# A decoder step on one core: 28 instead of 20 blocks of u split by ScalarE and GpSimd, and dots ordered behind the one-hot rows

## The chip, the cores and the metric

The kernel runs on one core of one Trainium2 chip. The metric is the device time of one execution in microseconds (us), from three runs of the kernel before. Engine names are those of the profile: PE is TensorE, PEld its weight loads, DVE is VectorE, ACT is ScalarE, POOL is GpSimd, SP is SyncE. SP and POOL also issue transfers (DMA); those issued by one engine go out in its order.

## The reference

One inference step of a decoder with two layers, for a prompt group and a small sample group. Layer 0 mixes tokens with a delta rule and a linear recurrence, layer 1 with windowed attention. After each mixer comes the same block, PEER, and the change lies in it alone:

```python
def block(tb):                                             # 128 tokens and more
    q = (tb @ w_q).reshape(PEER_BLOCK, PEER_HEADS, 2, PEER_D_SUB)
    s = jnp.einsum('thcd,hcnd->thcn', q, sub_keys)         # 8 heads x 2 halves x 128 keys
    s_top, i_top = lax.top_k(s, PEER_TOPK)                 # 16 of each half
    cand = s_top[:, :, 0, :, None] + s_top[:, :, 1, None, :]
    best, pos = lax.top_k(cand, PEER_TOPK)                 # 16 experts of 16384 per head
    expert = take(cand_idx, pos); gate = softmax(best)
    act = gelu(einsum('td,thkd->thk', tb, u_tab[expert]))
    return einsum('thk,thkd->td', gate * act, v_tab[expert])
```

A token meets 128 experts, each with a row of u and a row of v of 1024 numbers.

## The kernel before

For three token tiles of 128 (384 columns) the kernel doesn't gather: it multiplies by the whole table u, in 128 blocks of 128 experts, masks the result with a dense gate matrix, and multiplies by the whole of v. For a fourth tile and the sample rows, experts are fetched by row (gathers) and reduced on DVE (dots). `peer(layer)` does this, once per layer, in stages.

**Scores.** 16 half-heads (hc): a projection by a block of w_q on PE, a float32 product with the keys (`psc`, line 445), copies by ACT (`q`, `scs`, `ss`), top-16 on DVE (`topk_half`, lines 267 to 271). Beside them, `presplit_load` and `presplit_pool` (lines 104 to 116) prepare the first NPOOL blocks of u: a matrix product in float32 accuracy takes each block as two float16 halves, high and low. SP loads the block (`gst`, three buffers), ACT scales it and copies the high half (into `gpr`, two buffers), POOL subtracts to get the low half (line 114), and SP stores both in DRAM (`PW`).

**Pairs and u steps.** A u step (`u_step`) is 24 matmuls of 128x384 on PE (`pu`, lines 91 to 93: high by high, high by low, low by high) and a gelu on ACT. Its block comes from `ublock` (line 143): one of the first NPOOL is loaded from PW, ready (`wpr`); a later one is loaded raw (`wst`), and ACT makes the high half (`wh`, line 77) and DVE the low half (`wl`, line 86) just ahead of PE. Three buffers hold `wst` and `wpr` together, two hold `wh` and `wl`. While PE does u steps, DVE forms the 50 candidate pairs of each token and head and takes the best 16 (`topk_pairs`, lines 267 to 318), first for the samples and the gathered tile, then for dense tile 0. It ends in `ij` (line 503); PE transposes it (`pt`), and DVE and ACT form `lt`.

**Gates.** Twelve stages, four for each dense tile. In one stage DVE writes 16 one-hot rows (`oh`, lines 530 to 533, in groups of four instructions, two buffers of groups), PE multiplies them in 64 small matmuls (`pg`, lines 537 and 538; 768 in all), ACT copies the results to `stage`, and 2 MB go to DRAM (`GD`). Each stage has u steps in the program beside it (UG 3), and the pairs of the next dense tile come after stages 3 and 7. After each stage three steps of `g_ustep` follow (GU 3): one gather on POOL (line 390, 512 KB, three buffers `row`) and, from the third step on, one dot on DVE (line 397). That gives 36 gathers and 34 dots in the gates, 10 of the dots in stages 0 to 3 and 24 in stages 4 to 11.

**Main.** 128 blocks of v with the rest of the u steps; `yps` (line 654) is its product. 79 u steps and two matmuls of the next come before its first matmul.

What stands in which order on an engine is not the order of the program: a scheduler simulates the engines and issues what it finds ready, so it may place a dot far ahead of the stage that it was written behind. `behind(ins)` (line 124) binds what is written under it to be issued behind given instructions, and `last_on(V)` is the last DVE instruction written so far.

Of the kernel before, what the change touches and what calls it, by code (L numbers as in the profile page):

```python
# [70 lines left out]
class Kern:  # L71
# [249 lines left out]
    def peer(self, layer):  # L321
        nc, tc, A = self.nc, self.tc, self.A
        V, S, G, T = nc.vector, nc.scalar, nc.gpsimd, nc.tensor
# [49 lines left out]
        def run_u(k):  # L373
            for _ in range(k):
                u_step()
# [11 lines left out]
        def gather(src, n):  # L387
            k = korder[n]
            r = rows[0].tile([P, D], F32, name="row")
            G.indirect_dma_start(out=r, out_offset=None, in_=src,  # L390
                                 in_offset=bass.IndirectOffsetOnAxis(ap=elist[:, k:k + 1], axis=0))
            return r

        def g_dot(n):
            k = korder[n]
            u = ubuf.pop(n)
            V.tensor_tensor_reduce(u, u, self.xtok[:, 0] if k < P else xrep, 1.0, 0.0, OP.mult, OP.add,  # L397
                                   hd[:, k:k + 1])
            if n % GRP == GRP - 1:
                a = korder[n - GRP + 1]  # L400
                S.activation(wgt[:, a:a + GRP], hd[:, a:a + GRP], AF.Gelu_apprx_tanh)
                V.tensor_mul(wgt[:, a:a + GRP], wgt[:, a:a + GRP], glist[:, a:a + GRP])

        def g_ustep():
            if gn[0] < NK:
                ubuf[gn[0]] = gather(urows, gn[0])
                gn[0] += 1
            if gn[1] < NK and gn[1] + 2 < gn[0] or gn[0] == NK and gn[1] < NK:
                g_dot(gn[1])
                gn[1] += 1  # L410
# [64 lines left out]
        with tc.tile_pool(name="gates", bufs=1, reuse_waits="tile") as gp, \  # L475
# [12 lines left out]
            def pairs(t):  # L488
                ev = tp.tile([P, 8, TOPK], F32, name="ev")
                gt = tp.tile([P, 8, TOPK], F32, name="gt")  # L490
                self.topk_pairs(tp, st[:, t], ix[:, t], P, 8, ev, gt)
                lts[t] = ev, gt

            def pairs_t(t):

                ev, gt = lts[t]
                ei = tp.tile([P, P], I32, name="ei")
                V.tensor_copy(ei, ev.rearrange("p a b -> p (a b)"))
                e2 = tp.tile([P, 2, P], I32, name="e2")
                V.tensor_scalar(e2[:, 0], ei, 7, None, op0=OP.logical_shift_right)  # L500
                V.tensor_scalar(e2[:, 1], ei, 127, None, op0=OP.bitwise_and)
                ij = tp.tile([P, 2, P], F32, name="ij")
                V.tensor_copy(ij, e2)
                pt = psum.tile([P, 4, P], F32, name="pt")
                T.transpose(pt[:, 0], ij[:, 0], self.ident)
                T.transpose(pt[:, 1], ij[:, 1], self.ident)
                T.transpose(pt[:, 2], gt.rearrange("p a b -> p (a b)"), self.ident)
                lt = tp.tile([P, 4, P], F16, name="lt", bufs=2)
                self.copy(lt[:, 0:2], pt[:, 0:2])
                V.tensor_scalar(lt[:, 2], pt[:, 2], SCG, None, op0=OP.mult)  # L510
                V.scalar_tensor_tensor(lt[:, 3], pt[:, 2], SCG, lt[:, 2], op0=OP.mult, op1=OP.subtract)
                lts[t] = lt

            def gates(t, part, us):

                lt = lts[t]
                stage = gp.tile([P, P, TG], F32, name="stage")
                run_u(us - 1)
                order = self.last_on(S)
                for t4 in range(0, TG, 4):  # L520
                    if t4 % 8 == 0:

                        sl = slice(part * TG + t4, part * TG + t4 + 8)

                        def tok(k):
                            return lt[:, k, sl].rearrange("p (a b) -> p a b", b=2)[:, :, None, :].to_broadcast([P, 4, P, 2])

                        io = self.iota2[:, None].to_broadcast([P, 4, P, 2])
                        oh = gp.tile([P, 4, 4, P, 2], F16, name="oh", bufs=2)
                        V.tensor_tensor(oh[:, 0], io, tok(1), op=OP.is_equal)  # L530
                        V.tensor_tensor(oh[:, 1], io, tok(0), op=OP.is_equal)
                        V.tensor_mul(oh[:, 2], oh[:, 1], tok(2))
                        V.tensor_mul(oh[:, 3], oh[:, 1], tok(3))
                    pg = psum.tile([P, 4, P], F32, name="pg", bufs=4)
                    for k in range(4):
                        q, r = divmod(t4 % 8 + k, 2)
                        T.matmul(pg[:, k], oh[:, 0, q, :, r], oh[:, 2, q, :, r], start=True, stop=False)
                        T.matmul(pg[:, k], oh[:, 0, q, :, r], oh[:, 3, q, :, r], start=False, stop=True)  # L538
                    with self.behind(order):
                        self.copy(stage[:, :, t4:t4 + 4].rearrange("p i t -> p t i"), pg)  # L540
                    order = []
                    if t4 == TG // 2:
                        run_u(1)
                nc.scalar.dma_start(GD[P // TG * t + part], stage)
# [20 lines left out]
            for k in range(12):  # L565
                gates(k // 4, k % 4, self.UG)
                acc[0] += self.GU
                while acc[0] >= 1:
                    g_ustep()
                    acc[0] -= 1  # L570
                if k % 4 == 3 and k < 11:
                    run_u(self.UP)
                    pairs(k // 4 + 1)
                    pairs_t(k // 4 + 1)
# [995 lines left out]
    def run(self):  # L1570
        nc, tc, A = self.nc, self.tc, self.A
        with ExitStack() as ctx:
            self.constants(ctx)
            self.RING, self.NSP, self.UG, self.GU, self.ROWS = 50, 32, 3, 3, 9
            self.UP = 7
            dp = ctx.enter_context(tc.tile_pool(name="scratch", bufs=1, space=bass.MemoryType.DRAM))
            self.GD = dp.tile([12, P, P, 32], F32, name="GD")
            self.NPRE, self.NPOOL = (0, 0), 20
            self.PW = dp.tile([2, max(self.NPRE) + self.NPOOL, P, 2, KB, P], F16, name="PW")
            self.AD = dp.tile([self.NSP, P, ND], F32, name="AD")  # L1580
            self.wst = ctx.enter_context(tc.tile_pool(name="wst", bufs=3))
            self.wsp = ctx.enter_context(tc.tile_pool(name="wsp", bufs=2))
            xp = ctx.enter_context(tc.tile_pool(name="x", bufs=1))
            self.xtok = xp.tile([P, 2, D], F32, name="xtok")
            self.xh = xp.tile([P, KB, NT], F16, name="xh")
            self.xl = xp.tile([P, KB, NT], F16, name="xl")
            self.eq = xp.tile([P, 2, 256], F32, name="eq")
            with tc.tile_pool(name="xin", bufs=1) as q:
                xT = q.tile([P, KB, NT], F32, name="xT")
                self.wfirst = {20: self.wblock(A["wab"][20])}  # L1590
                for kb in range(KB):
                    if kb == 4:
                        self.wfirst[4] = self.wblock(A["wab"][4])
                    nc.sync.dma_start(xT[:, kb], A["xT"][:, kb])
                    self.split(self.xh[:, kb], self.xl[:, kb], xT[:, kb])
            self.bd = dp.tile([16, P, LB], F32, name="bd")
            self.sbd = dp.tile([P, P], F32, name="sbd")
            xd0 = dp.tile([NT, D], F32, name="xd0")
            xd1 = dp.tile([3 * P, D], F32, name="xd1")
            self.xd = [A["xtok"], xd1]  # L1600
            with ExitStack() as c:
                pre = self.mixer_ab(c)
                self.presplit(pre, 0, self.NPRE[0])
            self.xd = [xd0, xd1]
            self.peer(0)
            with ExitStack() as c:
                pre = self.mixer_c(c)
                self.presplit(pre, 1, self.NPRE[1])
            self.peer(1)
# [141 lines left out]
```

## Time and profile before

| what | value |
|---|---|
| runs | 2965.84, 2963.49, 2955.86 us; median 2963.49 us |
| profiled execution, its own time | 2954.78 us |
| its span in the trace | 2953.1 us |
| PE busy | 2824.2 us (96%) |
| DVE busy | 2501.0 us (85%) |
| ACT busy | 1351.7 us (46%) |
| POOL busy | 956.7 us (32%) |
| moved | 811.33 MB, mean 275 GB/s |
| mean granted PE clock | 0.989 |
| chain that ended last | PE 59%, DMA 13%, DVE 12%, ACT 7%, issue 6% |

Busy shares are means over stages with different limits; a span outside the instructions of 1.7 us lies between the execution's own time and the trace. A matmul is in flight longer than its distance to the next (0.33 us against 0.16), so a busy PE isn't a PE at its peak: where PE's steps matter, distances of starts are taken. In layer 0 the scores lie at about 356 to 470 us, the pairs to 592, the gates to 835; `yps` begins at 852.3.

### The profile page before, as it was taken

How to read it: one execution, taken by the hardware profiler on the slowest of the kernel's cores; microseconds unless marked ns; L12 is line 12 of the kernel's file. 1: busy time of each engine (PE TensorE's matmuls, PEld its weight loads, DVE VectorE, ACT ScalarE, POOL GpSimd, SP SyncE). 2: the span in 40 equal slices, each digit the busy share in tenths (PEclk: the TensorE clock that was granted, in tenths of full speed). 3: DMA queues.
4: the chain of work that ended last, by engine and by line, in shares of the span. 5: the costliest groups of instructions: out<-in, count | busy, mean ns of one | idle time of the engine just before them, and what ended most of it. 6: DMA issues, size and time to landing. Idle time of an engine off the chain costs nothing.

```text
span 2953.1 us, 49153 instructions
## 1 busy us (share of the span) xinstructions
PE 2824.2 (96%) x18198; PEld 1714.9 (58%) x18198; DVE 2501.0 (85%) x5483; ACT 1351.7 (46%) x2127; POOL 956.7 (32%) x702
## 2 busy tenths in 40 slices
PE   8999999899999999999998999989999999999998
PEld 7787686466655555544447658646665555554443
DVE  6755789999878898889985869999988889888998
ACT  4733473266743333333435747236674333333332
POOL 2300151310034554445530014140005455444652
PEclk9999999999999999999999999999999999999999
DMA  4223495975699999999984348686569999999996
GB/s 134 71 83 129 147 330 193 311 253 199 225 380 357 372 362 369 360 324 375 354 289 162 106 144 299 238 296 223 211 252 382 355 374 363 355 347 346 330 368 223
DMA packets 320324, 811.33 MB, mean 275 GB/s; under 512 B 28099, under 2 KB 150411, under 8 KB 316244
## 3 DMA queue, kind: packets, MB, share of 16 engines
q1 hardware_dynamic: 229228, 455.37, 44.7%
q0 software_dynamic: 78336, 285.25, 26.0%
q10 hardware_dynamic: 12520, 67.58, 6.2%
q8 instruction: 142, 2.33, 0.3%
q14 instruction: 98, 0.80, 0.1%
HBM read 707.25 MB, written 99.46 MB: 273 GB/s over the span
## 4 chain that ended last, share of the span: by engine, by line
PE 59%; DMA 13%; DVE 12%; ACT 7%; issue 6%; POOL 3%; ACTq 0%; SPq 0%; POOLq 0%; DVEq 0%
PE yps L654 24%; PE pu L93 7%; PE pu L91 7%; PE pu L92 7%; DMA row<-in_u_rows,elist 3%; DMA gl<-GD 3%; ACT stage L77 2%; POOL row L390 2%; DMA gst<-in_uT 1%; DVE row L397 1%; ACT wh L77 1%; DVE wl L86 1%; PE psg L1034 1%; DMA row<-in_v_rows 1%; PE pg L538 1%
## 5 line engine op out<-in xcount | busy, mean ns | idle before, releaser
L654 PE MATMUL yps<-vv,vw 128*128 128x512 f16 x4536 | 1008.4, 380 | 10.4 <-DVE vv L86 8.4
L654 PEld LDWEIGHTS <-vw 128*128 128x128 f16 x4608 | 450.7, 98 | 546.1 <-issue 19.6
L390 POOL DMA_INDIRECT row<-in_v_rows,elist x272 | 398.1, 1463 | 836.3 <-ACT stage L77 425.0
L93 PE MATMUL pu<-xh,wl 128*128 128x384 f16 x1728 | 565.8, 329 | 28.5 <-DVE wl L86 28.1
L91 PE MATMUL pu<-xh,wh 128*128 128x384 f16 x1728 | 567.5, 328 | 21.7 <-ACT wh L77 21.7
L92 PE MATMUL pu<-xl,wh 128*128 128x384 f16 x1728 | 566.9, 328 | 0.0
L390 POOL DMA_INDIRECT row<-in_u_rows,elist x272 | 385.8, 1418 | 509.5 <-DVE yac L592 129.3
L86 DVE SCALAR_TENSOR_TENSOR wl<-wst,wh 128x1024 f16<-128x1024 f32 x284 | 351.3, 1240 | 165.8 <-ACT wh L77 151.7
L77 ACT ACTIVATE wh<-wst 128x1024 f16<-128x1024 f32 x284 | 299.3, 1054 | 403.5 <-PE pu L92 293.3
L77 ACT ACTIVATE vv<-row 128x1024 f16<-128x1024 f32 x252 | 264.2, 1051 | 369.6 <-PE yps L654 291.7
L91 PEld LDWEIGHTS <-wh 128*128 128x128 f16 x2816 | 279.9, 99 | 166.3 <-ACT wh L77 39.1
L93 PEld LDWEIGHTS <-wl 128*128 128x128 f16 x2816 | 277.5, 99 | 168.5 <-DVE wl L86 38.5
L86 DVE SCALAR_TENSOR_TENSOR vv<-row,vv 128x1024 f16<-128x1024 f32 x252 | 307.7, 1222 | 63.6 <-ACT vv L77 60.2
L92 PEld LDWEIGHTS <-wh 128*128 128x128 f16 x2816 | 277.7, 99 | 132.8 <-issue 5.9
L592 DVE SCALAR_TENSOR_TENSOR yac<-row,wgt,yac 128x1024 f32<-128x1024 f32 x268 | 343.3, 1281 | 8.7 <-DMA row<-in_v_rows,elist 6.7
L397 DVE CUSTOM_DVE_ANT_0 row<-row,xtok 128x1024 f32<-128x1024 f32 x256 | 308.4, 1220 | 20.7 <-DMA row<-in_u_rows,elist 20.5
L77 ACT ACTIVATE vw<-act 128x384 f16<-128x384 f32 x256 | 129.3, 514 | 226.8 <-PE yps L654 191.5
L77 ACT ACTIVATE stage<-pg 128x512 f32<-128x512 f32 x192 | 182.7, 1104 | 71.1 <-DMA GD<-stage 42.9
L366 ACT ACTIVATE act<-pu 128x384 f32<-128x384 f32 x256 | 121.7, 477 | 87.0 <-PE pu L93 86.1
L84 DVE TENSOR_TENSOR vw<-act,vw 128x384 f16<-128x384 f32 x256 | 139.3, 553 | 13.8 <-ACT vw L77 13.4
L640 DVE TENSOR_TENSOR act<-act,gl 128x384 f32<-128x384 f32 x256 | 127.6, 552 | 11.2 <-DMA gl<-GD 9.1
L92 PE MATMUL pq<-xl,wh 128*128 128x264 f16 (+1 forms) x480 | 132.9, 277 | 0.7 <-DVE xl L84 0.7
(502 smaller groups left out, 4138.8 us busy)
## 6 DMA issues: line engine op xcount, KB each, us to landing
row<-in_v_rows SPq DMA_DIRECT2D x256, 512.0 KB
wst<-in_uT SPq DMA_DIRECT2D x216, 512.0 KB
GD<-stage ACTq DMA_DIRECT2D x24, 2048.0 KB
gl<-GD SPq DMA_DIRECT2D x64, 768.0 KB
gst<-in_uT SPq DMA_DIRECT2D x40, 512.0 KB
PW<-gpr SPq DMA_DIRECT2D x40, 512.0 KB
wpr<-PW SPq DMA_DIRECT2D x40, 512.0 KB
wst<-in_wq SPq DMA_DIRECT2D x32, 512.0 KB
```

Of the source, the lines that this page charges most:

```text
L77: self.nc.scalar.activation(out, in_, AF.Copy, scale=scale)
L84: eng.tensor_sub(lo, src, hi)
L86: eng.scalar_tensor_tensor(lo, src, scale, hi, op0=OP.mult, op1=OP.subtract)
L91: mm(out, wh, xh, start=start, stop=False)
L92: mm(out, wh, xl, start=False, stop=False)
L93: mm(out, wl, xh, start=False, stop=stop)
L366: S.activation(t, ps[:, 0:ND], AF.Gelu_apprx_tanh, scale=1.0 / SCW)
L390: G.indirect_dma_start(out=r, out_offset=None, in_=src, in_offset=bass.IndirectOffsetOnAxis(ap=elist[:, k:k + 1], axis=0))
L397: V.tensor_tensor_reduce(u, u, self.xtok[:, 0] if k < P else xrep, 1.0, 0.0, OP.mult, OP.add, hd[:, k:k + 1])
L592: V.scalar_tensor_tensor(dst, vbuf.pop(n), wgt[:, k:k + 1], dst, op0=OP.mult, op1=OP.add)
L640: V.tensor_mul(a6, a6, gl)
L654: T.matmul(yps[t][:, o], w[:, a, c], v[:, b, o], start=x == 0 and k == 0, stop=x == P - 1 and k == 2)
```

## The change

NPOOL goes from 20 to 28. Blocks 20 to 27 of u are then prepared in the scores by ACT and POOL and read from PW, and no longer split by ACT and DVE in front of their u step. And what DVE does in the `g_ustep` calls behind gate stages 4 to 11 is bound behind the last DVE instruction of that stage, its last one-hot product (line 533). The gathers themselves, on POOL, are not bound, and stages 0 to 3 not either.

```diff
--- before.py
+++ after.py
@@ -566,7 +566,8 @@
                 gates(k // 4, k % 4, self.UG)
                 acc[0] += self.GU
                 while acc[0] >= 1:
-                    g_ustep()
+                    with self.behind(self.last_on(V) if k >= 4 else []):
+                        g_ustep()
                     acc[0] -= 1
                 if k % 4 == 3 and k < 11:
                     run_u(self.UP)
@@ -1575,7 +1576,7 @@
             self.UP = 7
             dp = ctx.enter_context(tc.tile_pool(name="scratch", bufs=1, space=bass.MemoryType.DRAM))
             self.GD = dp.tile([12, P, P, 32], F32, name="GD")
-            self.NPRE, self.NPOOL = (0, 0), 20
+            self.NPRE, self.NPOOL = (0, 0), 28
             self.PW = dp.tile([2, max(self.NPRE) + self.NPOOL, P, 2, KB, P], F16, name="PW")
             self.AD = dp.tile([self.NSP, P, ND], F32, name="AD")
             self.wst = ctx.enter_context(tc.tile_pool(name="wst", bufs=3))
```

Three places show how the order of the engines changes, in layer 0; layer 1 is alike. Rows give the line, the operation and output<-input.

ACT, end of the scores, before: `q`, `scs` and `ss` of the last half-heads, then the table and the first gelu of a u step.

```order
L77 ACTIVATE q<-pq 128x256
L77 ACTIVATE q<-pq 128x264
L77 ACTIVATE scs<-psc 128x512
L77 ACTIVATE ss<-psc 128x8
L77 ACTIVATE q<-pq 128x256
L77 ACTIVATE q<-pq 128x264
L77 ACTIVATE scs<-psc 128x512
L77 ACTIVATE ss<-psc 128x8
L77 ACTIVATE scs<-psc 128x512
L77 ACTIVATE ss<-psc 128x8
L366 ACT_TABLE_LOAD
L366 ACTIVATE act<-pu 128x384
```

ACT at the same place now:

```order
L77 ACTIVATE q<-pq 128x256
L77 ACTIVATE q<-pq 128x264
L77 ACTIVATE gst<-gst 128x1024
L77 ACTIVATE scs<-psc 128x512
L77 ACTIVATE ss<-psc 128x8
L77 ACTIVATE gpr<-gst 128x1024
L77 ACTIVATE gst<-gst 128x1024
L77 ACTIVATE gpr<-gst 128x1024
L366 ACT_TABLE_LOAD
L366 ACTIVATE act<-pu 128x384
L77 ACTIVATE scs<-psc 128x512
L77 ACTIVATE ss<-psc 128x8
```

Before, the last `gpr` stands four half-heads earlier; now two blocks go in each of these half-heads, and the last `scs` stands behind the first gelu instead of ahead of it.

DVE, the first one-hot rows of stage 0, before (`wl` is a low half, L397 a dot):

```order
L86 SCALAR_TENSOR_TENSOR wl<-wst,wh 128x1024
L269 MATCH_REPLACE cwork<-best_7597,cand_7568 128x50
L510 TENSOR_SCALAR lt<-pt 128x128
L530 TENSOR_TENSOR oh<-iota_65,lt 128x1024
L531 TENSOR_TENSOR oh<-iota_65,lt 128x1024
L530 TENSOR_TENSOR oh<-iota_65,lt 128x1024
L531 TENSOR_TENSOR oh<-iota_65,lt 128x1024
L270 MAX best_7597<-cwork 128x8
L511 SCALAR_TENSOR_TENSOR lt<-pt,lt 128x128
L397 ISA row,hd<-row,xtok 128x1024
L397 ISA hd 128x1
L532 TENSOR_TENSOR oh<-oh,lt 128x1024
```

DVE, the same place now:

```order
L290 TENSOR_TENSOR cand_8782<-st 128x8x8
L304 CAST pf_7667<-pos_7622 128x128
L510 TENSOR_SCALAR lt<-pt 128x128
L530 TENSOR_TENSOR oh<-iota_65,lt 128x1024
L531 TENSOR_TENSOR oh<-iota_65,lt 128x1024
L530 TENSOR_TENSOR oh<-iota_65,lt 128x1024
L531 TENSOR_TENSOR oh<-iota_65,lt 128x1024
L311 TENSOR_TENSOR eq_7669<-pf_7667,lperm 128x256
L316 TENSOR_REDUCE gsum_7685<-gexp_7664 128x8
L511 SCALAR_TENSOR_TENSOR lt<-pt,lt 128x128
L267 MAX best_8811<-cand_8782 128x8 x8
L532 TENSOR_TENSOR oh<-oh,lt 128x1024 x2
```

Between the last top-16 of the scores and the first row L530 there stood 29 dots and 8 `wl`; now there are 10 dots and no `wl`. The first `wl`, that of block 28, comes 28 one-hot instructions later.

DVE, the last one-hot rows of the seventh stage (stage 6), before:

```order
L530 TENSOR_TENSOR oh<-iota_65,lt 128x1024
L531 TENSOR_TENSOR oh<-iota_65,lt 128x1024
L503 CAST ij<-e_8857 128x256
L532 TENSOR_TENSOR oh<-oh,lt 128x1024
L533 TENSOR_TENSOR oh<-oh,lt 128x1024
L530 TENSOR_TENSOR oh<-iota_65,lt 128x1024
L531 TENSOR_TENSOR oh<-iota_65,lt 128x1024
L532 TENSOR_TENSOR oh<-oh,lt 128x1024
L533 TENSOR_TENSOR oh<-oh,lt 128x1024
L86 SCALAR_TENSOR_TENSOR wl<-wst,wh 128x1024
L510 TENSOR_SCALAR lt<-pt 128x128
L530 TENSOR_TENSOR oh<-iota_65,lt 128x1024
```

DVE, the last one-hot rows of the same stage now:

```order
L530 TENSOR_TENSOR oh<-iota_65,lt 128x1024
L531 TENSOR_TENSOR oh<-iota_65,lt 128x1024
L532 TENSOR_TENSOR oh<-oh,lt 128x1024
L533 TENSOR_TENSOR oh<-oh,lt 128x1024
L397 ISA row,hd<-row,xtok 128x1024
L397 ISA hd 128x1
L397 ISA row,hd<-row,xtok 128x1024
L397 ISA hd 128x1
L397 ISA row,hd<-row,xtok 128x1024
L397 ISA hd 128x1
L86 SCALAR_TENSOR_TENSOR wl<-wst,wh 128x1024
L530 TENSOR_TENSOR oh<-iota_65,lt 128x1024
```

Three dots now stand in a row behind the last L533 of a stage, ahead of the next `wl` and the next stage's rows. Counted to the `wl` of block 53: before, 88 one-hot instructions, 36 dots, 33 `wl` and 358 others since the scores; now 136, 22, 25 and 364.

## Rows read from the trace of the kernel before

**Rows 1.** Windows: us; busy of PE, PEld, DVE, ACT, POOL (count); clock; DMA share; GB/s.

```profile
356.00:470.00 114.00, 109.94 (x947) 94.55 (x948) 98.66 (x537) 75.98 (x124) 43.40 (x21) 0.99 0.70 254
835.00:1250.00 415.00, 411.27 (x2183) 213.61 (x2182) 364.07 (x453) 158.33 (x225) 206.44 (x146) 1.00 1.01 367
```

**Rows 2.** Windows, instructions of tile `pu` alone (PE, PEld, DVE, ACT), both layers.

```profile
458.50:852.30 393.80, 326.36 (x1898) 0.00 (x0) 0.00 (x0) 37.38 (x79) 0.98 0.73 258
540.00:592.00 52.00, 39.02 (x207) 0.00 (x0) 0.00 (x0) 4.27 (x9) 0.87 0.88 297
...
1851.00:2244.80 393.80, 324.41 (x1898) 0.00 (x0) 0.00 (x0) 37.39 (x79) 0.99 0.73 258
```

**Rows 3.** PE, product of main: shortest, median, longest ns; first and last start.

```profile
L654 PE MATMUL yps<-vv,vw x4536: 376/379/632, 852.3 to 2942.4; 128*128 128x512 f16 x198
```

**Rows 4.** PE's timeline: start, us, line, operation, output<-input.

```profile
599.73 0.33 PE L92 MATMUL pu<-xl,wh 128*128 128x384 f16 x1
...
601.84 0.33 PE L93 MATMUL pu<-xh,wl 128*128 128x384 f16 x1
...
551.17 0.52 PE L91 MATMUL pu<-xh,wh 128*128 128x384 f16 x1
551.49 0.53 PE L92 MATMUL pu<-xl,wh 128*128 128x384 f16 x1
...
771.05 0.22 PE L537 MATMUL pg<-oh 128*128 128x128 f16 x1
771.11 0.22 PE L538 MATMUL pg<-oh 128*128 128x128 f16 x1
```

**Rows 5.** PE's waits 458 to 853 us: us in all, times, longest.

```profile
PE pu L93 <- DVE wl L86: 13.6, 8, 5.7
PE pu L91 <- ACT wh L77: 10.9, 12, 2.2
```

**Rows 6.** Window of 10 us in the pairs, columns as in the first group.

```profile
546.00:556.00 10.00, 5.12 (x17) 2.37 (x18) 9.46 (x19) 0.95 (x1) 4.15 (x4) 0.50 0.82 303
```

**Rows 7.** DVE's timeline: dot, low half, one-hot rows, low half of block 53.

```profile
543.31 1.21 DVE L397 CUSTOM_DVE_ANT_0 row<-row,xtok 128x1024 f32<-128x1024 f32 x1
544.46 0.08 DVE L397 DVE_READ_ACCUMULATOR2_ANT hd<- 128x1 f32 x1
...
549.60 1.22 DVE L86 SCALAR_TENSOR_TENSOR wl<-wst,wh 128x1024 f16<-128x1024 f32 x1
550.74 1.32 DVE L313 TENSOR_TENSOR eq<-eq,ce 128x1120 f32<-128x1120 f32 x1
...
587.34 0.68 DVE L530 TENSOR_TENSOR oh<-iota,lt 128x1024 f16<-128x1024 f16 x1
587.94 0.68 DVE L531 TENSOR_TENSOR oh<-iota,lt 128x1024 f16<-128x1024 f16 x1
...
715.00 1.23 DVE L86 SCALAR_TENSOR_TENSOR wl<-wst,wh 128x1024 f16<-128x1024 f32 x1
```

**Rows 8.** ACT's timeline: first and last presplit copy, last `scs`.

```profile
359.62 1.05 ACT L77 ACTIVATE gst<-gst 128x1024 f32<-128x1024 f32 x1
...
437.51 1.08 ACT L77 ACTIVATE gpr<-gst 128x1024 f16<-128x1024 f32 x1
...
463.53 0.60 ACT L77 ACTIVATE scs<-psc 128x512 f32<-128x512 f32 x1 [4.15 <-issue]
```

**Rows 9.** Windows, line 86 alone: busy of DVE, clock, DMA share, GB/s of all.

```profile
366.00:436.00 70.00, 14.55 (x10) 1.00 0.94 339
438.00:463.00 25.00, 2.42 (x2) 1.00 0.29 98
```

**Rows 10.** DVE groups, 366 to 436 us, then 438 to 463: busy, mean ns, idle before.

```profile
L86 DVE SCALAR_TENSOR_TENSOR wl<-wst,wh 128x1024 f16<-128x1024 f32 x10 | 14.6, 1456 | 6.9 <-ACT wh L77 6.8
...
L269 DVE MATCH_REPLACE8 swork<-st,scs 128x128 f32<-128x128 f32 x40 | 11.0, 275 | 0.0
...
L269 DVE MATCH_REPLACE8 swork<-st,scs 128x128 f32<-128x128 f32 x20 | 5.6, 279 | 0.0
...
L86 DVE SCALAR_TENSOR_TENSOR wl<-wst,wh 128x1024 f16<-128x1024 f32 x2 | 2.4, 1210 | 0.0
```

## The prediction

> **What bounds the kernel now.** I read the windows by stage first. In main PE is busy 411.27 of 415 us and the DMA share is 1.01 [rows 1]; neither edit changes what main does, so whatever is won or lost lies ahead of the first product of main, at 852.3 us [rows 3]. In the scores, PE has 109.94 of 114 us and ACT only 75.98 [rows 1]. The stretch from the scores' end to main holds 1898 u matmuls in 393.80 us, and in layer 1 the same number in the same time [rows 2], so I work on layer 0 and double.
>
> What that stretch would take if PE never waited comes from the distances of starts in PE's timeline. Fourteen consecutive u matmuls start from 599.73 to 601.84, which is 2.11 / 13 = 0.1623 us each, and a small gate matmul 0.06 [rows 4]. So 1898 x 0.1623 + 768 x 0.06 = 308 + 46 = 354 us, against 393.8: some 40 us a layer are lost (up to 4 of them are the last key scores). Where? Between 540 and 592, just after the twenty ready blocks end, 207 matmuls need 33.6 us and take 52 [rows 2]: 18.4 lost in one place. The waits name the reason: PE waits 13.6 us on DVE's low halves, one time 5.7, and 10.9 on ACT's high halves [rows 5]. After the long wait the granted clock is 0.50, the 1.2 GHz level, over a 10 us slice [rows 6], and u matmuls start 0.32 us apart [rows 4]: a wait costs more than its length. DVE is busy 9.46 of 10 us in that slice [rows 6]: it isn't late by a wait of its own but has too much to do there.
>
> **The change, part by part.** *DVE ahead of the one-hot rows.* By the orders shown, 19 dots and 8 low halves leave the way to the first one-hot row. A dot holds DVE 1.15 us (543.31 to 544.46) and a low half 1.14 (549.60 to 550.74) [rows 7]: 21.9 + 9.1 = 31.0 us. The first row, now at 587.34 [rows 7], would start at 556.3, if the scores ended as before.
>
> *The scores.* Eight more blocks go through ACT, POOL and DMA. Twenty take from 359.62 to 438.6, the end of the last copy [rows 8], which is 3.9 us each; eight more make 31.6 and end at 470.2. The last `scs` was at 463.53, after a gap of 4.15 us on ACT [rows 8]; such a gap stands in each half-head once the blocks are through. The copies themselves (8 x 2.1 = 16.9 us) just fill four such gaps. The transfers, 16 x 0.52 = 8.4 MB, need 24.7 us at the 339 GB/s of the pool stretch, where now, from 438 to 463, only 98 GB/s move [rows 9], and POOL has 43.40 of 114 us to do [rows 1]. So most is covered. What isn't: the copies stand ahead of `q` and `scs` in ACT's order, and wait there for their loads and stores. No row shows four half-heads with two blocks each. From below: the cover holds, 0. From above: the last `scs` and the top-16 behind it come after the last copy and one landing, some 10 us late. I take s = 5 for DVE, near what the tail passes 463.5 by (470.2 - 463.5 = 6.7). The first one-hot row then starts at 561.3. PE fills such delays in part with u steps that need neither ACT's split nor DVE's, and I charge it nothing beyond that.
>
> On SP's queue, the 8 loads and 8 stores more stand ahead of or among the loads of the first ready blocks; that is priced as the last rival. The 8 loads of `wpr` in place of `wst` are of one size.
>
> *Dots behind the rows.* They are not gone: 24 come back in stages 4 to 11, three in a row. So the low halves after block 28 are late again, and here the gain is cut. From the first one-hot row to the low half of block 53, before, lie 715.0 - 587.34 = 127.7 us [rows 7], with 88 one-hot instructions, 7 dots, 25 low halves and 115 small ones. Now it is 136, 12, 25 and 106: 48 x 0.60 + 5 x 1.15 = 28.8 + 5.8 more, less 9 small ones of an estimated 0.3 (a low estimate from their kinds in the pairs), so 31.9 more: 159.6 us. (0.60 is 587.34 to 587.94 [rows 7].) The low half of block 53 starts at 561.3 + 159.6 = 720.9, 6 us later than now; but PE has far less left then: 26 u steps of 24 (101.3 us) and 14 groups of 16 small matmuls (13.4), where before 26 groups (25.0) were left. 720.9 + 114.7 = 835.6. The same count for block 28 bounds PE less: 28 one-hot instructions and 52 small ones, some 32 us, put its low half at 593.7; 51 u steps (198.7) and 41 groups (39.4) from there end at 831.8. PE would come to block 28 earlier than that and wait there, and again on the way to 53; after it, it leads.
>
> *After block 53.* Before, 852.3 - 715.0 - 126.3 = 11.0 us are lost there, by waits on the halves and at the hand-over to main. Nothing in the change speaks to the hand-over; 24 dots stand among these stages. Bounds 0 and 11; I take 5, since what remains for PE alone is mostly u steps whose low halves DVE can do at 1.14 us against PE's 3.90. So main starts at 840.6.
>
> **Sum.** 852.3 - 840.6 = 11.7 us a layer, 23.4 in both. Against the profiled execution's 2954.78 that is 2931.4; its execution lies 8.7 under the median of the runs shown, 2963.49, against which I predict 2940.
>
> A rule of the Trainium skill speaks against the first edit. Low halves take 1456 ns in the pool stretch against 1210 ns just after it, while MATCH_REPLACE takes 275 and 279 [rows 10]. GPSIMD Engine Reference, section "1. Specifications", says that GpSimd shares its SBUF interfaces with VectorE and contends with DVE instructions of two SBUF inputs. By the rows only the low halves pay, two in the last half-heads, 0.5 us a layer; by the rule read widely (all of DVE 20% slower beside 17.2 us of POOL's work) it would be 3.4 us a layer, 7 in all. The sum above needs neither.
>
> **Rivals.** *All of it is won.* If the scores' cover holds (s = 0) and nothing is lost after block 53, each layer gains 11.7 + 5 + 5 = 21.7, and the time is 2963.5 - 43.4 = 2920. For it: 18.4 lost in one place that the ready blocks now pass. Against: the low half of 28 is still behind the one-hot rows.
>
> *The gain is given back.* With s = 10 and again 11 us lost after 53, 11.7 - 5 - 6 = 0.7 a layer: 2962, no change. For it: the DMA at 0.94 in the pool stretch [rows 9], and DVE without a gap; the stalls would only have moved from block 20 to block 28.
>
> *Slower.* The loads of the first ready blocks stand on SP behind stores that wait for POOL's subtraction, which waits for ACT's copies, which wait for loads. If the tail closes that ring, the first u steps wait for `wpr`, PE stands at the scores' end, its clock falls to 1.2 GHz as in [rows 6], and everything behind it is late. It decides when the scores' end slips by 16.7 us with 5 lost later, or 10.7 with 11 lost. At 17 and 11 it is 11.7 - 12 - 6 = -6.3 a layer, 2976. Against: the queue had idle DMA behind the blocks, 0.29 [rows 9].
>
> That the change doesn't do what it says is excluded by the orders: the eight low halves are gone there and the dots stand behind line 533.
>
> **How the numbers follow.** The forecast has 0.48 (its own range 2926 to 2954), all of it won 0.18, given back 0.21, slower 0.13. A measurement of this kernel can tell about 0.3%, 8.9 us. Faster: nearly all of the first, all of the second and a tenth of the third, 0.67. Same: most of the third and a little of the others, 0.20. Slower: 0.13. The range reaches from beyond the best rival, 2915, to the one without change, 2964.
>
> **What would show it.** In the profile after: the first one-hot row near 561, no long wait of PE between 540 and 580, new waits on `wl` near 585 to 600, the low half of block 53 near 721, `yps` near 841, the last `scs` at 464 to 474. It is wrong if PE waits in the scores for `q` or `wpr` by more than some us, if DVE still waits for gathers behind the stages (a dot in front of one-hot rows would then hold PE), or if the stall after 540 was not DVE's load but something that stays.

## The result: 4.2% slower, and where the profile shows it

The changed kernel takes 3085.61 us in the median of six runs; the kernel before, on the same chip, 2963.56. The ratio is 1.0415, with a 95% interval of 1.0395 to 1.0435. The forecast was 2940, its range 2915 to 2964.

From the first key score to the first product of main, before took 486.5 us in either layer; now it is 528.1 and 524.7. Main, counted from there to the first product of its five last blocks, took 678.0 and 679.0 us; now 694.9 and 705.8. So 80 us are lost ahead of main and 44 in it.

The first product of main, which answers to [rows 3] (line numbers behind 570 are one higher now):

```profile
L655 PE MATMUL yps<-vv,vw x4536: 376/379/634, 898.8 to 3073.1; 128*128 128x512 f16 x198
```

It comes 46.5 us later than before. The u matmuls alone, by windows as in [rows 2]; the last line is the kernel before in the third window:

```profile
538.80:578.80 40.00, 33.02 (x190) 0.00 (x0) 0.00 (x0) 3.71 (x8) 0.96 0.55 175
598.80:618.80 20.00, 11.67 (x53) 0.00 (x0) 0.00 (x0) 1.00 (x2) 0.83 0.51 165
698.80:758.80 60.00, 39.94 (x217) 0.00 (x0) 0.00 (x0) 4.87 (x10) 0.94 0.69 250
798.80:818.80 20.00, 9.41 (x49) 0.00 (x0) 0.00 (x0) 1.00 (x2) 0.91 0.84 308
838.80:898.80 60.00, 46.75 (x241) 0.00 (x0) 0.00 (x0) 4.97 (x11) 0.86 1.05 383
...
698.80:758.80 60.00, 49.05 (x290) 0.00 (x0) 0.00 (x0) 5.67 (x12) 1.00 0.56 202
```

Count the need at 0.1623 us for each u matmul, as in the prediction, and 0.06 for each small gate matmul beside them; what a window has beyond that is lost. From 538.8 to 578.8, the place of the old stall, 190 need 30.8 of 40 us: that stall shrank to 9 us. From 598.8 to 618.8 stands the wait at block 28, 20 - 8.6 - 3.7 = 7.7 lost with the mean clock at 0.83. But from 698.8 to 758.8, where the kernel before lost nothing (290 and 224 small ones need all of the 60), 217 (and 168 small) need 45.3 of 60; from 798.8 to 818.8 it is 10.8 of 20; and from 838.8, at the hand-over to main (from the last gate matmul to main's first product), 241 need 39.1 of 60. These last three lose 45 us.

PE's waits up to the first product, as in [rows 5]:

```profile
PE pu L91 <- ACT wh L77: 28.4, 12, 4.2
PE pg L537 <- ACT stage L77: 6.6, 5, 4.8
PE pu L93 <- DVE wl L86: 6.2, 6, 2.3
```

The low halves, 13.6 us before, fell to 6.2. The high halves, 10.9 before, rose to 28.4: ACT is late more often than DVE now. What holds ACT is among its waits from 590 to 850 us (us in all, times, longest). In the kernel before:

```profile
ACT stage L77 <- DMA GD<-stage: 21.2, 7, 4.9
ACT stage L77 <- PE pu L92: 12.0, 3, 4.0
```

In the changed kernel:

```profile
ACT stage L77 <- DMA GD<-stage: 38.8, 9, 10.4
```

The first copy of a stage waits for the store of the stage before (which ACT issues itself) to leave the one buffer. The three waits that the profile puts down to a u matmul end 7.2 us behind the store, like the 4.0 us wait just ahead of them that it puts down to the store, so they are the store's too: 33.2 us before against 38.8. The sum has hardly grown; what has grown is the single wait, the longest from 4.9 to 10.4 us. One such place in the changed kernel, put together from the timelines of POOL, ACT and PE:

```profile
735.30 1.68 POOL L390 DMA_INDIRECT row<-in_u_rows,elist  x1 [17.55 <-DVE hd L397]
737.28 1.99 POOL L390 DMA_INDIRECT row<-in_u_rows,elist  x1 [0.30 <-issue]
739.58 1.43 POOL L390 DMA_INDIRECT row<-in_u_rows,elist  x1 [0.30 <-issue]
...
740.07 0.33 ACTq L544 DMA_DIRECT2D GD<-stage  x1
...
753.66 1.02 ACT L77 ACTIVATE stage<-pg 128x512 f32<-128x512 f32 x1 [7.30 <-DMA GD<-stage]
754.49 1.99 ACT L77 ACTIVATE wh<-wst 128x1024 f16<-128x1024 f32 x2
...
755.60 0.50 PE L91 MATMUL pu<-xh,wh 128*128 128x384 f16 x1 [4.20 <-ACT wh L77]
```

Three gathers are issued from 735.3 to 741; the store of 2 MB goes out at 740.07; the next stage's copy can start only at 753.66, 13.6 us behind the store, and the two high halves stand behind it on ACT. PE waits 4.20 us for the first, and the matmul after it takes 0.50 us: the granted clock is 0.50 from 755.6 to 757.5, the 1.2 GHz level. Before, POOL issued no gather between 606.6 and 818.2 us, and eleven of the twelve stores of the layer lie there:

```profile
603.52 1.22 POOL L390 DMA_INDIRECT row<-in_v_rows,elist  x1 [2.34 <-DVE hd L397]
605.04 1.54 POOL L390 DMA_INDIRECT row<-in_v_rows,elist  x1 [0.30 <-issue]
818.18 0.94 POOL L390 DMA_INDIRECT row<-in_v_rows,elist  x1 [211.60 <-ACT stage L77]
...
726.54 0.33 ACTq L544 DMA_DIRECT2D GD<-stage  x1
...
735.87 2.90 ACT L77 ACTIVATE stage<-pg 128x512 f32<-128x512 f32 x3 [3.25 <-DMA GD<-stage]
```

There the copy starts 9.3 us behind the store, the latest of the ten copies of that layer that wait for one (6.5 to 9.3). The Trainium skill (DMA: Bandwidth & Descriptors, section "Issuing engines are not separate DMA queues") says that transfers started by different engines run on the same 16 DMA engines and interleave; the trace agrees, with 13.6 us beside POOL's gathers against 9.3 without.

Main's loss has its place too: in layer 0, 100 us that begin 400 us behind main's first product and hold its last u steps, in windows with the columns of [rows 1]. In the kernel before:

```profile
1252.00:1352.00 100.00, 99.09 (x473) 45.79 (x472) 84.32 (x120) 37.07 (x53) 49.22 (x26) 1.00 0.98 334
```

In the changed kernel:

```profile
1299.00:1399.00 100.00, 86.93 (x408) 40.09 (x407) 70.58 (x102) 31.96 (x46) 29.66 (x20) 0.97 0.88 290
```

The timelines of DVE and then POOL in the changed kernel, there: each dot waits for its gather, the low half of a v block (`vv`) stands behind it, and the next gather is issued only when a dot or an accumulation has given its buffer back.

```profile
1327.13 1.23 DVE L397 CUSTOM_DVE_ANT_0 row<-row,xtok 128x1024 f32<-128x1024 f32 x1 [4.50 <-DMA row<-in_u_rows,elist]
...
1328.28 1.02 DVE L641 TENSOR_TENSOR act<-act,gl 128x384 f32<-128x384 f32 x2
1329.22 1.22 DVE L86 SCALAR_TENSOR_TENSOR vv<-row,vv 128x1024 f16<-128x1024 f32 x1
...
1333.46 1.23 DVE L397 CUSTOM_DVE_ANT_0 row<-row,xtok 128x1024 f32<-128x1024 f32 x1 [1.61 <-DMA row<-in_u_rows,elist]
...
1334.61 1.22 DVE L86 SCALAR_TENSOR_TENSOR vv<-row,vv 128x1024 f16<-128x1024 f32 x1
...
1320.63 1.68 POOL L390 DMA_INDIRECT row<-in_u_rows,elist  x1 [5.65 <-DVE yac L593]
1328.63 1.01 POOL L390 DMA_INDIRECT row<-in_u_rows,elist  x1 [6.33 <-DVE hd L397]
1334.96 1.68 POOL L390 DMA_INDIRECT row<-in_u_rows,elist  x1 [5.32 <-DVE hd L397]
```

### The profile page after: what moved, and what is told of

The parts are those of the page before. It is cut to its first block, busy times and chain, and to the rows that moved or that the text cites. A ratio compares the mean times of both kernels' runs of the same rounds, so it can differ in the third digit from the quotient of the medians.

```text
span 3083.7 us, 49209 instructions
## 1 busy us (share of the span) xinstructions
PE 2872.1 (93%) x18198; PEld 1732.3 (56%) x18198; DVE 2494.1 (81%) x5467; ACT 1367.0 (44%) x2143; POOL 931.8 (30%) x718
## 5 line engine op out<-in xcount | busy, mean ns | idle before, releaser
L390 POOL DMA_INDIRECT row<-in_u_rows,elist x272 | 370.6, 1362 | 942.9 <-DVE hd L397 673.4
L91 PE MATMUL pu<-xh,wh 128*128 128x384 f16 x1600 | 531.7, 332 | 57.8 <-ACT wh L77 57.6
L93 PE MATMUL pu<-xh,wl 128*128 128x384 f16 x1600 | 528.2, 332 | 14.5 <-DVE wl L86 14.4
L92 PE MATMUL pu<-xl,wh 128*128 128x384 f16 x1600 | 531.2, 332 | 0.0
L390 POOL DMA_INDIRECT row<-in_v_rows,elist x272 | 368.6, 1355 | 518.2 <-DVE yac L593 212.5
L86 DVE SCALAR_TENSOR_TENSOR wl<-wst,wh 128x1024 f16<-128x1024 f32 x268 | 334.4, 1249 | 153.9 <-ACT wh L77 152.9
L77 ACT ACTIVATE wh<-wst 128x1024 f16<-128x1024 f32 x268 | 282.0, 1054 | 361.0 <-PE pu L92 262.0
L91 PEld LDWEIGHTS <-wh 128*128 128x128 f16 x2688 | 269.4, 100 | 199.1 <-ACT wh L77 77.0
L397 DVE CUSTOM_DVE_ANT_0 row<-row,xtok 128x1024 f32<-128x1024 f32 x256 | 309.3, 1223 | 65.2 <-DMA row<-in_u_rows,elist 64.8
L92 PEld LDWEIGHTS <-wh 128*128 128x128 f16 x2688 | 267.1, 99 | 127.8 <-issue 10.2
L91 PE MATMUL pu<-xh,wpr 128*128 128x384 f16 x448 | 148.7, 332 | 9.8 <-DMA wpr<-PW 6.3
L114 POOL TENSOR_TENSOR gpr<-gst,gpr 128x1024 f16<-128x1024 f32 x56 | 121.6, 2172 | 111.2 <-ACT gpr L77 109.6
```

Source lines behind the costliest of these rows:

```text
L77: self.nc.scalar.activation(out, in_, AF.Copy, scale=scale)
L86: eng.scalar_tensor_tensor(lo, src, scale, hi, op0=OP.mult, op1=OP.subtract)
L91: mm(out, wh, xh, start=start, stop=False)
L92: mm(out, wh, xl, start=False, stop=False)
L93: mm(out, wl, xh, start=False, stop=stop)
L114: self.nc.gpsimd.tensor_sub(o[:, 1], st, o[:, 0])
```

## The experiments

All are read by three lengths in one profile each (us): from first key score to first product of main, the gates alone in layer 0 (first one-hot row to last gate matmul), and main, in layers 0 and 1. Between the first key score and main stand 78 or 79 u steps of 3.9 us, so a difference of one step between two kernels is part of these lengths. "Ring of 42" is explained at the two stage buffers, "rows" under main; the profile of the two stage buffers is of an execution of 2996.8 us, the longest of its five.

| kernel | time | ratio to before, 95% | to main, L0 / L1 | gates | main, L0 / L1 |
|---|---|---|---|---|---|
| before | 2963.6 | | 486.5 / 486.5 | 232.8 | 678.0 / 679.0 |
| both edits | 3085.6 | 1.0395 to 1.0435 | 528.1 / 524.7 | 263.1 | 694.9 / 705.8 |
| first alone (28 blocks) | 2977.9 | 1.003 to 1.0061 | 493.4 / 487.8 | 239.1 | 683.1 / 685.5 |
| second alone (dots bound) | 3038.8 | 1.0233 to 1.0288 | 516.4 / 518.7 | 263.9 | 679.4 / 697.2 |
| both, bound from stage 8 | 3008.3 | 1.0131 to 1.0177 | 503.4 / 507.4 | 243.4 | 684.2 / 682.3 |
| both, 24 blocks | 3028.0 | 1.0126 to 1.0312 | 507.2 / 505.4 | 258.3 | 677.0 / 702.6 |
| 28, no late gathers | 3005.1 | one run | 493.1 / 490.4 | 231.0 | 687.6 / 693.5 |
| both, short late dots | 3078.4 | 1.0254 to 1.0525 | 504.7 / 507.1 | 238.1 | 716.7 / 712.2 |
| both, two stage buffers | 2986.8 | 1.0034 to 1.009 | 497.4 / 501.4 | 243.0 | 683.1 / 683.1 |
| both, ring of 42 alone | 3064.8 | 1.0301 to 1.0384 | 526.6 / 524.1 | 266.2 | 682.6 / 698.6 |
| before, two stage buffers | 2962.0 | 0.9976 to 1.0008 | 479.1 / 490.2 | 234.7 | 676.8 / 680.8 |
| first alone, two stage buffers | 2976.7 | 1.0023 to 1.007 | 486.7 / 499.1 | 232.0 | 682.0 / 678.7 |
| both, lag of 3 in main | 3085.8 | 1.0294 to 1.0535 | 527.5 / 527.4 | 265.0 | 701.7 / 700.3 |
| both, ring of 42, 11 rows | 3039.1 | 1.0212 to 1.0299 | 524.1 / 526.8 | 261.6 | 671.7 / 684.1 |
| before, ring of 42, 11 rows | 2989.4 | 1.006 to 1.0117 | 490.0 / 514.9 | 238.3 | 679.9 / 675.4 |
| both, two stage buffers, 11 rows | 2981.9 | 1.0037 to 1.0086 | 497.3 / 502.6 | 241.0 | 676.8 / 677.5 |
| before, two stage buffers, 11 rows | 2973.3 | 1.0015 to 1.0046 | 478.4 / 503.3 | 234.7 | 682.7 / 676.7 |

**Which edit.** One edit at a time, and the second one halved:

```diff
# first alone, against the kernel before
-            self.NPRE, self.NPOOL = (0, 0), 20
+            self.NPRE, self.NPOOL = (0, 0), 28
# second alone, against the kernel before
-                    g_ustep()
+                    with self.behind(self.last_on(V) if k >= 4 else []):
+                        g_ustep()
# second halved, against both edits
-                    with self.behind(self.last_on(V) if k >= 4 else []):
+                    with self.behind(self.last_on(V) if k >= 8 else []):
```

> The first edit alone: 28 blocks split in the scores, dots free as before. Theory A (the second edit costs: 24 dots and their 512 KB gathers now fall into gate stages 4 to 11, beside the 2 MB gate stores, so that ACT's stage copies wait longer for the store and the high halves behind them are late): no more than about 10 us off before, 2945 to 2975, and the longest wait of a stage copy on a gate store about 5 us as before. Theory B (the first edit costs: eight more blocks lengthen the scores and everything behind is late): 3040 or more. Theory C (each costs a part): about 3020.

> The second edit alone: 20 blocks, dots of stages 4 to 11 bound behind the one-hot rows. Theory A: most of the loss is here, 3040 to 3090. Theory B: near before, 2945 to 2975. Theory C: about 3020.

> Both edits, but only the dots of stages 8 to 11 bound (12 of 24). Theory A: about half the loss, 3000 to 3040. Theory B: as both edits, 3075 to 3095.

The second edit alone costs 76 us, the first 15, half of the second with the first 45. Theory A stands for most of it, though the first alone lies 3 us above its range and the second 1 us below; B falls. But the parts add up to 91 and not to 122. With 24 blocks:

> Both edits with 24 blocks instead of 28. The second edit alone (20 blocks) measured 3038.8, both 3085.6. If more blocks make the second edit dearer because the gate stages then come sooner and tighter: about 3060. If the two just add (first edit alone plus 15): 3045 to 3050.

It is 3028, which meets neither expectation and isn't clear of the 3038.8 with 20 (the intervals overlap). So the loss doesn't grow steadily with the blocks. That it hangs on the order that the scheduler makes of each number is a guess; no run tests it.

**Are the late gathers the cause, or the tighter stages?** The gathers and dots of stages 4 to 11 go to main:

```diff
-                acc[0] += self.GU
+                acc[0] += self.GU if k < 4 else 0
                 ...
-                    with self.behind(self.last_on(V) if k >= 4 else []):
+                    with self.behind([]):
```

> 28 blocks, and the gathers and dots of stages 4 to 11 are not there but left to main (nothing of the result is left out). The order of one-hot rows and low halves in the gates is nearly that of both edits (block 53 behind 136 one-hot instructions). Main has 24 gathers more per layer and takes longer, so the first product of main is what counts: at 852 before, 899 with both edits. Theory A with the gathers' transfers or the dots as the cause: 830 to 850. If instead the tighter order of the gate stages itself makes stage copies wait for the store: 880 to 900. The whole time is then not below 2960, since main's DMA is full.

The first product came at 865.9, between the two ranges, with the first key score at 372.8 instead of 365.8. The way to main is 493 and 490 us against 528 and 525, the gates 231. So 35 of the 42 us lost ahead of main in layer 0 come with the late gathers and dots, and the tighter order without them costs little: 7 and 4 us a layer.

**Transfers or dots?**

```diff
-            V.tensor_tensor_reduce(u, u, self.xtok[:, 0] if k < P else xrep, ...)
+            e = 8 if short[0] else D                  # short[0] holds in stages 4 to 11
+            V.tensor_tensor_reduce(u[:, 0:e], u[:, 0:e], (self.xtok[:, 0] if k < P else xrep)[:, 0:e], ...)
```

> Both edits, but the 24 dots of gate stages 4 to 11 read 8 of 1024 columns (the rest of those dots is left out), so that DVE gives them about 0.1 us instead of 1.15 and the gathers still come behind the same one-hot rows. Read by the first product of main: 852 before, 899 with both edits, 866 with no late gathers and dots at all. If the gathers' transfers beside the gate stores are the cost: 885 to 900, and the stores still land 9 to 14 us after their issue. If DVE's time for the dots is the cost (24 x 1.07 = 26 us): 866 to 875.

The first product came at 872.2, as DVE's time would have it: the gates are 25 us shorter. Yet the stores behave otherwise too. With the dots short, four of the late stores of layer 0 went out 2.0 to 6.0 us after the last gather instruction had ended, and ACT's copy started 7.0 to 8.9 us behind them; the two with a gather ending in the last 1.1 us took 10.2 and 12.0. So this run took away both suspects at once and doesn't part them. And main grew to 717 and 712 us, so the whole time hardly fell.

Take the four kernels with late gathers so far (both edits, the second alone, bound from stage 8, short dots) and those copies of layer 0 that the profile has waiting for the store. Where no gather was issued in the 12 us before the store, or the last one had ended 3.4 us or more before it, the copy started 6.6 to 9.4 us behind the store. Where the last one ended at most 2.1 us before the store, or after its issue, it was 8.9 to 14.5. (In layer 1 the ranges overlap more: up to 10.5 without a gather near, from 8.3 with one.)

**The wait itself.** Two stage buffers, with room made for them:

```diff
-                stage = gp.tile([P, P, TG], F32, name="stage")
+                stage = gp.tile([P, P, TG], F32, name="stage", bufs=2)
-            self.RING, self.NSP, ... = 50, 32, 3, 3, 9
+            self.RING, self.NSP, ... = 42, 40, 3, 3, 9
```

> Both edits, with two buffers instead of one for a gate stage's result, so that ACT's first copy of a stage need not wait for the store of the stage before. To make room, the ring of finished u steps has 42 places instead of 50 and 8 more of them go through DRAM; 2 u steps fewer stand ahead of main (7.8 us). If ACT's wait for the store, with the high halves behind it, is what the late gathers cost: ACT's waits for the store fall from 38.8 us to under 5 and the first product of main comes at 855 to 875 (7.8 of it from the two steps). If DVE's load is the cost: 885 to 895.

> The control of the two stage buffers: both edits, one stage buffer, and only the ring of 42 places with 40 u steps through DRAM. If the second buffer brought the gain: from the first key score to the first product of main about 520 to 530 us (528 with both edits, 497 with two buffers), and 3060 or more in all. If the smaller ring did: near 2987, with main at 683.

The control with the ring alone is at 3064.8, with the second buffer 2986.8: 78 us for a buffer. Both came as the theory of the wait had them, with the first product at 868.0 and 897.7. (The ring alone brings 21 us, nearly all in main; with two buffers 78 u steps stand ahead of main and not 79, which is 3.9 of the 29 us below.) No wait for a store is left among ACT's waits, the gates fall from 266 to 243 us, the way to main by 29 and 23 us, and main in layer 1 from 698.6 to 683.1. PE's waits for high halves up to the first product, with the ring alone and then with two buffers:

```profile
PE pu L91 <- ACT wh L77: 26.8, 11, 6.8
...
PE pu L91 <- ACT wh L77: 8.8, 4, 4.5
```

PE's u matmuls in the kernel with two buffers, in the 60 us of which both edits lost 15:

```profile
698.80:758.80 60.00, 48.32 (x282) 0.00 (x0) 0.00 (x0) 5.46 (x12) 1.00 0.73 264
```

282 instead of 217, at clock 1.00. Gathers and full dots are still there, so DVE's time for the dots isn't what the gates lose. By stretches, counted as in the windows above (us, layer 0 / layer 1):

| kernel | lost from first to last gate matmul | lost from there to main |
|---|---|---|
| before | 7.5 / 9.4 | 7.4 / 7.6 |
| both edits | 37.7 / 37.7 | 21.2 / 20.8 |
| both, ring of 42 alone | 35.5 / 30.5 | 21.3 / 20.9 |
| both, two stage buffers | 9.8 / 10.7 | 21.1 / 18.9 |
| 28, no late gathers | 11.8 / 10.7 | 14.2 / 14.8 |

So the pair shows that the one buffer, with ACT's wait for the store and the high halves behind it, carries nearly all of what the gates lose beyond the kernel before, and hardly any of what is lost behind them, at the hand-over to main. There both edits leave 11.1 u steps instead of 6.3 (two buffers 9.3), at a DMA share of 1.05 against 1.03; why each costs more wasn't tested. And one thing the pair doesn't separate: with a second buffer the scheduler also places the u steps otherwise, up to two steps sooner or later against a gate stage.

Does it hold back the kernels without late gathers as well?

> The kernel before with two stage buffers and the ring of 42. There the stores land 6.5 to 9.3 us after issue and no gathers lie beside them; ACT waits 21 us a layer for them but PE hardly. If the store is dear only beside the gathers: within 10 us of before, 2955 to 2975. If ACT's wait was a hidden bound of before too: 2930 to 2950.

> The first edit alone (15 us slower than before) with two stage buffers and the ring of 42. ACT waited 39.9 us for stores in a layer there. If that ate the gain of the 28 blocks: 2930 to 2955, faster than before. If the first edit's loss is in the scores, at the hand-over and in main: 2965 to 2985.

No: 2961.97 (ratio 0.9976 to 1.0008), and 2976.7 with 28 blocks, as without the second buffer. With 28 blocks and one buffer ACT waits 39.9 us for stores in layer 0, as much as with both edits, but no longer than 6.1 us at a time. So the sum of these waits doesn't tell their price: of these kernels the store is dear only where gathers make single waits long.

**Main.** Two theories, the dots' lag and the row buffers:

```diff
+        lag[0] = 3                                   # e11, in main; 2 before
-            self.RING, self.NSP, ..., self.ROWS = 50, 32, 3, 3, 9
+            self.RING, self.NSP, ..., self.ROWS = 42, 40, 3, 3, 11   # e16
```

> Both edits, and in main alone a dot or an accumulation follows its gather by three gathers instead of two. Main took 678.0 and 679.0 us in the two layers before, 694.9 and 705.8 with both edits. Theory M1 (main's program is the same, but DVE's order in it came out other, with dots too near behind their gathers, and v's low halves wait behind them): 678 to 688 in both layers. Theory M2 (main is longer for another reason, transfers or what the gates leave behind): 692 to 708.

> Both edits, one stage buffer, the ring of 42, and in main 11 instead of 9 buffers for rows of v and gathers. Theory M3 (main is longer because gathers wait for buffers that dots and accumulations give back late): main 675 to 685 in both layers, against what the ring of 42 alone gives. If buffers aren't it: as the ring of 42 alone.

The lag did nothing (701.7 and 700.3, the whole 3085.8): M1, as put, fell. More buffers took 11 and 14 us off main against the ring alone (671.7 and 684.1), and 26 off the whole. Whether they bind anyway:

> The kernel before with the ring of 42 and 11 buffers for rows in main. If main is bound by these buffers in before too: main 665 to 672 instead of 678, 2940 to 2955. If the buffers only count where dots and accumulations are late (as with both edits): main 674 to 680, 2955 to 2970.

> Both edits with two stage buffers (2987 measured) and 11 buffers for rows (26 us off the ring of 42 alone). If these are the two causes and independent: 2960 to 2972. If a loss at the hand-over to main stays that neither touches: 2975 to 2990.

> The kernel before with two stage buffers and 11 buffers for rows: the candidate. If the buffers bind main in before: 2935 to 2955. Otherwise 2955 to 2970.

In the kernel before they don't help: main is 679.9 and 675.4, as expected, but the whole is 2989.4 (1.006 to 1.0117), outside both ranges, and the loss lies ahead of main in layer 1 (514.9 us). With both repairs the changed kernel has main at 676.8 and 677.5, as before, and 2981.9 in all; some 18 us stay, on the way to main (497 and 503 us). The kernel before with both is 2973.3 (1.0015 to 1.0046), above both ranges, again with a longer way to main in layer 1 (503.3). What lengthens that way when only buffers of main are added wasn't found. No version here beats the kernel before.

## Why the prediction was wrong, step by step

*DVE ahead of the one-hot rows: right, 4.9 us short.* The first row started at 571.1, with the whole layer 4.9 us later from its first key score on; 566.2 against 561.3 predicted. But PE had only 23.6 u steps done at the first gate matmul instead of 28.1, so that of the 20 us by which the gates begin sooner some 2 are won for PE.

*The scores: right in size.* From first to last key score it is 100.5 us instead of 97.4, for s = 5. The low halves beside POOL took 1449 ns in the mean and MATCH_REPLACE 275, as in [rows 10]. The Trainium skill (GPSIMD Engine Reference, section "1. Specifications") names contention with GpSimd for DVE instructions with two SBUF inputs; the trace agrees for the low halves (1210 ns without POOL in [rows 10]), and the prediction's wider reading, all of DVE 20% slower, doesn't hold.

*The wait at block 28: right.* 7.7 us are lost there, with the clock lower. The low half comes at 605.6 instead of 593.7.

*DVE up to block 53: mis-sized.* Its low half came at 744.3, not 720.9; 4.9 of it is the start, 4.9 the first row. Of the other 13.6, 8.3 are DVE waiting (11.1 us in that stretch against 2.8 before, for ACT's high halves and PE's gate matmuls), which my sum of durations couldn't hold; the remaining 5.3 are in the durations, where the nine small instructions fewer saved nothing.

*After block 53: the step that failed.* I took 5 us lost with 11 as the upper end, "since what remains for PE alone is mostly u steps whose low halves DVE can do at 1.14 us against PE's 3.90". From 744.3 to 898.8 are 154.5 us against 114.7 of work: 39.8 lost. I weighed the moved dots on DVE alone. The gathers in front of them, which the program doesn't bind, moved as well, each held by a dot through the three buffers, and landed beside the 2 MB stores; ACT, at 46% busy, I left out of this term, though its stage copies wait for those stores with one buffer and the high halves stand behind them. Both could be seen in the trace of before: the waits of up to 4.9 us for a store, 33.2 in all, and POOL without a gather from 606 to 818 us. That is the part ahead of the last gate matmul, some 19 of the 39.8. The other 21 are lost at the hand-over, of which I wrote that nothing in the change speaks to it: five u steps more are left there than before, and two stage buffers don't mend it. Its cause stays open.

*"Neither edit changes what main does": failed.* Its program is the same, its order isn't (DVE's work in main stands in another order in each of the variants compared), and it was 16.9 and 26.8 us longer; I had put that at nothing without a reason. The smaller ring alone brings layer 0 to 683 and two stage buffers then layer 1, too; with more row buffers as well it is 677. So it depends on the ring, on what the gates leave behind and on the buffers of gathers. Which instruction begins it wasn't found.

*The rivals.* The slower one named the right direction in the wrong place: PE's waits for `wpr` were 3.0 us against 1.8. "Given back", with the stall moved from 20 to 28, is near what the first edit does alone: the one-hot rows start 6 and 8 us sooner behind the first key score, and gates, hand-over and main lose that and more, 15 us in all. Why these stay wasn't settled; two stage buffers don't mend it.

## What to carry to other kernels

When work is moved, follow the transfers that it releases: a dot bound to a place binds the gathers behind its buffers too, and the question is what else transfers then. Look for the in-order engine that waits for the slowed transfer and for what stands behind that wait; neither its busy share, here 46%, nor the sum of its waits told what that cost; the length of the single wait did. And where a scheduler decides the order, "the rest stays as it is" is a term to be bounded, not a premise.

## What the runs showed of the hardware that was not expected

A store of 2 MB whose buffer ACT's copy was waiting for was done in 6.5 to 9.4 us at most with no gather near it, and in 8.9 to 14.5 when the last of three gathers of 512 KB had been issued just before it or just after (layer 0). The two stores of the result section, from issue to copy, before and then changed, with what each DMA queue moved (q10 has the stores, q1 SP's transfers, q0 the gathers):

```profile
726.54:735.87 9.33, 9.33 (x73) 6.04 (x70) 9.33 (x18) 2.87 (x4) 0.00 (x0) 1.00 0.96 352
...
q10 hardware_dynamic: 144, 2.10, 63.7%
q1 hardware_dynamic: 327, 1.17, 31.6%
...
740.07:753.66 13.59, 11.33 (x89) 7.33 (x87) 8.06 (x13) 1.93 (x3) 0.94 (x1) 1.00 0.92 344
...
q10 hardware_dynamic: 144, 2.10, 36.1%
q1 hardware_dynamic: 417, 1.52, 32.9%
q0 software_dynamic: 288, 1.05, 22.5%
```

The DMA engines are nearly full in both, at about the same rate (352 and 344 GB/s); the second stretch is longer by what else moves in it, 1.4 MB more, which at 344 GB/s are an estimated 4.1 of the 4.3 us. The windows of 20 and 60 us around such places, in the result section, hide this: their DMA share is only 0.69 to 0.84.
